# A decoder kernel whose instructions are recorded, list-scheduled on a model of the engines, and emitted in that order

## The chip, the cores and the metric

The kernel runs on one core of one Trainium2 chip. The metric is the device time of one execution in microseconds (us), the median of several runs. A profile of one execution goes with it. TensorE (PE) does the matmuls and loads their weights (PEld); VectorE (DVE), ScalarE (ACT) and GpSimd (POOL) do the elementwise work; SyncE (SP) and ScalarE issue the transfers (DMA). Every engine works through its own queue in order, and waits on semaphores for what other engines make.

## The reference

A trunk of two layers on x, 2048 tokens by 1024 channels. Layer 0 is a gated delta rule (GDN) with 8 heads, layer 1 gated linear attention (GLA) with 4 heads; in both a head has 128 key and 256 value channels. Cut to what matters:

```python
for i in range(DEPTH):                                   # 2 layers
    y = gdn_mixer(x, ...) if i % 2 == 0 else gla_mixer(x, ...)
    x = layer_norm(DEEP_ALPHA * x + y, ln_g[i], ln_b[i])

def gdn_mixer(x, w_in, conv_w, a_log, dt_bias, norm_w, w_out):
    p = x @ w_in                                         # q, k, v, gate, beta, decay
    qkv = causal_conv_silu(p[..., :GDN_QKV], conv_w)     # 4 taps
    ...                                                  # l2norm of q and k, beta, log decay g
    o = gated_delta_rule(q, k, v, g, beta)               # a triangular solve per chunk, a state per head
    o = gated_rmsnorm(o, norm_w, gate)                   # times silu(gate)
    return o.reshape(B, T, GDN_VAL) @ w_out
```

`gla_mixer` has the same frame: x @ w_in, a recurrence with a decay for every key channel, the gated norm, and w_out.

## The kernel before, in words

**Tiling.** Tokens are cut into four groups of 512 (`TG`), each of four chunks of 128. A *phase* is one layer on one group; `PHASES` puts them in the order (0,0) (0,1) (1,0) (0,2) (1,1) (0,3) (1,2) (1,3). A *unit* is one head of a phase: 32 units of GDN and 16 of GLA. Products with weights are made in full precision from two halves: a tile is split into a high part and the rest (`split`: a ScalarE cast, then a subtraction on VectorE, or on GpSimd for the input weights), and three matmuls (`mm3`) replace one.

**Stages of a unit.** The *GEMM* stage multiplies x (`xh`, `xl`, one set of 8 slots for a phase) by the head's columns of w_in, which stream as 128-row chunks (`wraw`, split into `wh`, `wl`), into PSUM banks `g` (three): q and k (`kq`), values (`vt`), gate (`sg`). GDN adds the short convolution, three multiply-adds on VectorE (`acc`). The *prep* stage makes the chunk-local matrices in PSUM banks `c` (three). In GDN it solves a triangular system: a 16x16 block step of some 30 small VectorE operations (`X`, `Xt`) on a tile `Arep`, which is `X` written to DRAM (`blk`) and read back replicated; then matmuls. The *chain* stage runs the recurrence over the four chunks, in bank `h` (one) and `c`, with the state `S` updated by VectorE. The *out* stage multiplies the normed result (`oT`, split into `oth`, `otl`) by the head's rows of w_out (`woraw`, split into `woh`, `wol`) in bank `o` (one, `pso` in the profile), and VectorE adds each product to `y`. After the last head of a phase comes the layer norm, and in layer 0 the transposed result is written for layer 1 (`x2T`).

**What sets the order.** The four stages are four generators (`chains`, `preps`, `outs`, `gemms`). `Plan` keeps rough costs (`COST`: each result 0.8 us late), and `Plan.run` takes, at each step, the first generator whose step is due by these. This sets the order of emission, which is the urgency that the framework's own scheduler goes by when it orders each engine's queue. By hand are: a gap between the output products (`O_GAP`), a delay for loading `y` (`Y_WAIT`), a loader of output weights that runs ahead (`prefetched`, `WO_AHEAD`), and loads of the next phase's x in the last gate GEMM (`free`). The raw tiles of output weights, of x and of the layer norm's vectors (`load_gb`) share four `woraw` buffers.

All instructions are issued through one helper, line 121, so the profile tells them apart by tiles.

Of the kernel before, what the change touches and what calls it, by code (L numbers as in the profile page):

```python
# [49 lines left out]
class Plan:  # L50
    """Decides the order of emission, which is the scheduler's order of urgency: a rough model of the engines says
    when a step's operands are there, and of the steps that could go, that of the first thread goes."""

    def __init__(self):
        self.clock = 0.0
        self.events = {}
        self.busy = dict.fromkeys("vsgd", 0.0)
        self.done, self.used, self.opens, self.slots = {}, {}, {}, {}

    def tile(self, tag, ap, bufs):  # L60
        slots = self.slots.setdefault(tag, [])
        slots.append(ap.tensor.name)
        self.opens[slots[-1]] = self.used.get(slots[-1 - bufs], 0.0) if len(slots) > bufs else 0.0

    def ready(self, *tiles):
        names = [t[:].tensor.name for t in tiles]
        return max(max(self.done.get(n, 0.0), self.opens.get(n, 0.0)) for n in names)

    def note(self, key, aps):
        dst, src = aps[0], aps[1:]  # L70
        names = [a.tensor.name for a in aps]
        t = max([self.opens.get(names[0], 0.0)] + [self.done.get(n, 0.0) for n in names[1:]])
        n = 1
        for k in (src[-1] if key == "t" else dst).shape[1:]:
            n *= k
        psum = any(a.space == PSUM for a in aps)
        if key == "t":
            m = 1
            for k in src[0].shape[1:]:
                m *= k  # L80
            rate = 0.6 if src[0].dtype == F32 else 2.4
            cost = m / 1.2 if src[0] is src[-1] else max(n / rate, m / rate, 107 if rate > 1 else 53)
            self.clock = end = max(self.clock, t) + cost
            end += COST["t"]
        else:
            if key == "d":
                cost, wait = COST["d"], COST["dw"] + 4 * n * P / 200
            else:
                fixed, each = COST[key]
                cost, wait = fixed + n * each, COST["w"]  # L90
            begin = max(self.busy[key], t)
            self.busy[key] = max(self.busy[key], min(begin, self.clock)) + cost
            end = begin + cost + wait
        self.done[names[0]] = max(end, self.done.get(names[0], 0.0))
        for a in names:
            self.used[a] = max(end, self.used.get(a, 0.0))

    def run(self, *threads, start):
        def due(th):
            return self.events.get(th[1], 1e30) if isinstance(th[1], tuple) else th[1]  # L100

        threads = [[t, t0] for t, t0 in zip(threads, start)]
        while threads:
            th = next((th for th in threads if due(th) <= self.clock), None) or min(threads, key=due)
            assert due(th) < 1e30
            self.clock = max(self.clock, due(th))
            try:
                th[1] = next(th[0])
            except StopIteration:
                threads.remove(th)  # L110


class Planned:
    def __init__(self, plan, engine, key):
        self.plan, self.engine, self.key = plan, engine, key

    def __getattr__(self, name):
        op = getattr(self.engine, name)

        def call(*args, **kw):  # L120
            ins = op(*args, **kw)  # L121
            aps = [a for a in (*args, *kw.values()) if isinstance(a, bass.AP)]
            if name == "transpose":
                aps = [aps[0], aps[1], aps[1]]
            self.plan.note(self.key, aps)
            return ins
        return call


COST = {"v": (110, 1.04), "s": (110, 0.84), "g": (90, 2.35), "w": 800, "t": 200, "d": 450, "dw": 2000}  # L130
# [3 lines left out]
def trunk(ctx, tc, x, xT, w_in1, conv, a_log, dt_bias, nw1, w_out1, w_in2, gk_up, gk_b, nw2, w_out2,  # L134
          ln_g, ln_b, consts, out, phases=None):
    nc = tc.nc
    plan = Plan()
    v, s, g = (Planned(plan, e, k) for e, k in ((nc.vector, "v"), (nc.scalar, "s"), (nc.gpsimd, "g")))
    pe, sync, acts = Planned(plan, nc.tensor, "t"), Planned(plan, nc.sync, "d"), Planned(plan, nc.scalar, "d")
    ready, events = plan.ready, plan.events  # L140
# [10 lines left out]
    def T(tag, shape, bufs=1, dt=F32, p=None):  # L151
        count[0] += 1
        t = (p or sb).tile(list(shape), dt, tag=tag, name=f"{tag}_{count[0]}", bufs=bufs)
        plan.tile(tag, t[:], bufs)
        return t
# [87 lines left out]
    def after(*names):  # L243
        for name in names:
            yield name

    def mark(*name):
        events[name] = plan.clock

    def prefetched(specs, load, ahead=1):  # L250
        ready = []
        specs = iter(specs)

        def take(ahead=ahead):
            while len(ready) <= ahead:
                spec = next(specs, None)
                ready.append(None if spec is None else load(spec))
            return ready.pop(0)
        return take

    class Stream:
        def __init__(self, specs):
            self.specs = iter(specs)
            self.chunks = {}
            self.taken = self.loaded = 0

        def load(self, freed):
            while self.loaded < freed + W_BUFS:
                spec = next(self.specs, None)
                if spec is None:  # L270
                    return
                w, cols, kc = spec
                raw = T("wraw", [P, 272], RAW_BUFS)
                n = 0
                for c0, cn, pair in cols:
                    rows = w[kc * P:(kc + 1) * P]
                    if pair:
                        sync.dma_start(raw[:, :2 * cn].rearrange("p (a b) -> p a b", a=2),
                                       rows[:, :2 * pair].rearrange("p (a b) -> p a b", a=2)[:, :, c0:c0 + cn])
                        n = 2 * cn  # L280
                    else:
                        sync.dma_start(raw[:, n:n + cn], rows[:, c0:c0 + cn])
                        n += cn
                h = T("wh", [P, 272], W_BUFS, F32R)
                l = T("wl", [P, 272], W_BUFS, F32R)
                split(h[:, :n], l[:, :n], raw[:, :n], g)
                self.chunks[self.loaded] = h, l
                self.loaded += 1

        def take(self):  # L290
            self.taken += 1
            return self.taken - 1, self.chunks.pop(self.taken - 1)
# [16 lines left out]
    def gemm(xs, group, lags, done, free=None):  # L309
        d, chunks = [None] * len(lags), {}  # L310
        for i in range(KC + lags[-1]):
            for a, lag in enumerate(lags):
# [5 lines left out]
                if a == 0:  # L318
                    chunks[kc] = W.take()
# [628 lines left out]
```

## Time and profile before

| | |
|---|---|
| median of 3 runs | 3253.45 us (3251.26 to 3255.64) |
| profiled execution, first to last instruction | 3246.0 us |
| median less the profiled span | 7.5 us |
| instructions | 55,989 |
| TensorE busy | 3064.1 us, 94% |
| VectorE busy | 2466.0 us, 76% |
| ScalarE busy | 1565.6 us, 48% |
| GpSimd busy | 1127.2 us, 35% |
| mean granted TensorE clock | 0.983 |
| read and written | 269.86 and 26.28 MB |

The profiled execution's own time is its span, and what lies around the span is taken from the median. A group of instructions is told as: line, engine, operation, out<-in by tile names, shapes, count | busy us, mean ns of one | idle time of its engine just before them, and what ended that. A wait is told as: engine and tile that waited <- engine and tile that ended the wait: us in total, times, longest. Matmuls overlap in the array, and their ends are modelled, so TensorE's busy time is not time at its peak; the spacing of their starts in the timeline shows the rate.

### The profile page before, as it was taken

Reading aid. Unit: us, or ns where it says so; the run is one execution under the profiler, and the core shown is the slowest. Engines: PE = TensorE matmul, PEld = TensorE weight load, DVE = VectorE, ACT = ScalarE, POOL = GpSimd, SP = SyncE. Lnnn points to the kernel's source line nnn. Section 1 sums busy time; section 2 is a strip of 40 time slices with the busy share of each in tenths; the row PEclk is TensorE's granted clock in tenths of the full one; section 3 lists DMA queues with packets and bytes.
Section 4 is the critical chain, followed back from the end, with each engine's and each line's share of the span. In section 5 each row is a group of like instructions: output and inputs, shape, how many; then the busy total and the mean of one; then the engine's idle time right before and its main releaser. Section 6 shows DMA issues by size and latency. Waiting matters only on the chain.

```text
span 3246.0 us, 55989 instructions
## 1 busy us (share of the span) xinstructions
PE 3064.1 (94%) x18430; PEld 2601.6 (80%) x18430; DVE 2466.0 (76%) x6345; ACT 1565.6 (48%) x4099; POOL 1127.2 (35%) x1506
## 2 busy tenths in 40 slices
PE   8899999989999999998999999999899999899997
PEld 7688778768888888877887888978778878798885
DVE  7677788787877687688778768677877786866677
ACT  5445444445444456444444545553444454465542
POOL 5333333333233234334233324432433322433341
PEclk9899999999999999999999999999999999999998
DMA  6222223242222315324222322532422232243231
GB/s 179 63 77 74 78 73 98 82 147 76 74 78 78 101 53 153 109 79 127 80 79 82 92 73 67 153 98 78 136 77 74 82 94 69 78 137 97 66 125 59
DMA packets 311604, 299.83 MB, mean 92 GB/s; under 512 B 40544, under 2 KB 253792, under 8 KB 311312
## 3 DMA queue, kind: packets, MB, share of 16 engines
q1 hardware_dynamic: 285200, 278.42, 30.0%
q10 hardware_dynamic: 26112, 17.83, 1.9%
q8 instruction: 145, 2.38, 0.3%
q14 instruction: 147, 1.20, 0.1%
HBM read 269.86 MB, written 26.28 MB: 91 GB/s over the span
## 4 chain that ended last, share of the span: by engine, by line
PE 47%; DVE 20%; DMA 7%; issue 2%; ACT 2%; POOL 0%; SPq 0%; DVEq 0%; ACTq 0%; POOLq 0%
PE psg L121 24%; PE psc L121 10%; PE pso L121 10%; DMA Arep<-blk 5%; PE psh L121 4%; DVE X L121 3%; DVE D L121 2%; DVE y L121 2%; DVE acc L121 2%; DVE Xt L121 2%; DVE lntmp L121 1%; DMA blk<-X 1%; DVE z L121 1%; DVE lnrs L121 1%; DVE lnst L121 1%
## 5 line engine op out<-in xcount | busy, mean ns | idle before, releaser
L121 POOL TENSOR_TENSOR wl<-wraw,wh 128x256 fp32r<-128x256 f32 x1152 | 950.0, 843 | 1349.7 <-ACT wh L121 1207.9
L121 ACT CAST wh<-wraw 128x256 fp32r<-128x256 f32 x1152 | 444.6, 405 | 373.9 <-PE psg L121 229.2
L121 PE MATMUL psg<-wh,xh 128*128 128x256 f32 (+1 forms) x2048 | 609.5, 298 | 12.8 <-ACT acc L121 6.1
L121 PE MATMUL psg<-wl,xh 128*128 128x256 f32 (+1 forms) x2048 | 586.4, 286 | 2.7 <-POOL wl L121 2.5
L121 PE MATMUL psg<-wh,xl 128*128 128x256 f32 (+1 forms) x2048 | 585.7, 286 | 0.0
L121 PE MATMUL psg<-xh,wh 128*128 128x512 f32 x1280 | 525.6, 411 | 2.9 <-DVE vt L121 1.3
L121 PE MATMUL psg<-xl,wh 128*128 128x512 f32 x1280 | 518.8, 405 | 0.6 <-DVE xl L121 0.6
L121 PE MATMUL psg<-xh,wl 128*128 128x512 f32 x1280 | 514.8, 402 | 0.1
L121 PEld LDWEIGHTS psg<-wh,xh 128*128 128x128 f32 x2048 | 392.6, 192 | 30.4 <-ACT acc L121 6.9
L121 PEld LDWEIGHTS psg<-wl,xh 128*128 128x128 f32 x2048 | 393.3, 192 | 16.5 <-POOL wl L121 3.8
L121 PEld LDWEIGHTS psg<-wh,xl 128*128 128x128 f32 x2048 | 392.9, 192 | 1.0
L121 PE MATMUL pso<-woh,oth 128*128 128x512 f32 x736 | 326.3, 443 | 61.7 <-DVE y L121 55.7
L121 DVE SCALAR_TENSOR_TENSOR acc<-pb,taps,acc 128x512 f32<-128x512 f32 x384 | 330.1, 862 | 44.4 <-ACT acc L121 39.1
L121 DVE SCALAR_TENSOR_TENSOR y<-pso,z,y 128x512 f32<-128x512 f32 x368 | 273.6, 743 | 111.7 <-PE pso L121 109.2
L121 PE MATMUL pso<-woh,otl 128*128 128x512 f32 x736 | 304.8, 414 | 12.9 <-DVE otl L121 11.5
L121 PE MATMUL pso<-wol,oth 128*128 128x512 f32 x736 | 298.6, 406 | 0.0
L121 PEld LDWEIGHTS psg<-xh,wh 128*128 128x128 f32 x1280 | 243.9, 191 | 56.1 <-DVE sg L121 3.2
L121 PEld LDWEIGHTS psg<-xh,wl 128*128 128x128 f32 x1280 | 242.7, 190 | 54.7 <-POOL wl L121 1.0
L121 PEld LDWEIGHTS psg<-xl,wh 128*128 128x128 f32 x1280 | 243.4, 190 | 53.4 <-DVE xl L121 2.5
L121 ACT ACTIVATE junk<-psc 128x128 bf16<-128x128 f32 (+1 forms) x448 | 144.2, 322 | 185.4 <-PE psc L121 150.8
L121 PEld LDWEIGHTS pso<-woh,oth 128*128 128x128 f32 x736 | 140.2, 190 | 100.9 <-DVE y L121 72.0
L121 DVE TENSOR_TENSOR Xt<-Arep,X 128x60 f32<-128x60 f32 (+14 forms) x480 | 131.9, 275 | 84.7 <-DMA Arep<-blk 76.6
(192 smaller groups left out, 5459.0 us busy)
## 6 DMA issues: line engine op xcount, KB each, us to landing
wraw<-in_w_in SPq DMA_DIRECT2D x1152, 128.0 KB, 2.3
woraw<-in_w_out SPq DMA_DIRECT2D x192, 256.0 KB, 3.6
Arep<-blk SPq DMA_DIRECT2D x32, 512.0 KB
woraw<-in_xT SPq DMA_DIRECT2D x32, 256.0 KB, 3.2
y<-in_x SPq DMA_DIRECT2D x16, 512.0 KB, 4.3
Gb<-gcT ACTq DMA_DIRECT2D x32, 256.0 KB, 3.0
x<-y SPq DMA_DIRECT2D x32, 256.0 KB, 2.1
x2T<-th ACTq DMA_DIRECT2D x32, 256.0 KB, 4.4
```

Of the source, the lines that this page charges most:

```text
L121: ins = op(*args, **kw)
```

## The change

`Plan` and the generators go. Every engine call is first only recorded (`Recorder.note`), as an operation with its tiles, its cost, its dependencies and a priority: the rank of its stage (chain, prep, out, GEMM, in this order), then the order of recording. A tile is a *slot* out of a fixed set for its tag, given at the first operation that uses it, or already at the load when that names it with `also`. `Recorder.place` runs a list scheduler: five engines (VectorE, ScalarE, GpSimd, TensorE, SyncE) with a clock each; the engine that can start earliest takes, of the operations that are ready and have their slots, the one of best priority. Operations that need a new slot wait when their unit lies more than `HORIZON` units ahead of the first unit whose chain is unfinished. `Recorder.emit` issues the operations in the order placed, and `linearize=True` has the framework keep this order. x gets its own raw tiles (`xraw`, two), the layer norm's vectors their own (`gb`, four). The stages become plain functions, called unit by unit; `O_GAP`, `Y_WAIT`, the stream and the loader that runs ahead go. The diff, cut:

```diff
+    def note(self, engine, key, name, args, kw, also):
+        op = Op()
...
+        op.prio, op.unit = (self.rank, op.at), self.unit
...
+        for v in also:
+            v.of.given = op
+            op.fresh.append(v.of)
+        self.cost(op, dst, every)
...
+    def cost(self, op, dst, every):
...
         if key == "t":
...
+            if op.name == "transpose":
+                op.cost = 2 * dst.shape[0] / 2.4 + 4
+            elif every[1].dtype == F32:
+                op.cost = 4 * mov / 2.4 + 9
+            else:
+                op.cost = mov / 2.25 + 4.5
+            op.lag = 210
+        elif key == "d":
+            size = 4 * n * dst.shape[0]
+            op.cost, op.lag = 430, 1700 + size / 170
...
+        elif key == "v":
+            n = max(n, max(size_of(a.shape) for a in every))
+            took = (150 if psum else 160) + 1.04 * n
+            if op.name == "scalar_tensor_tensor":
+                took += 55
+            if len(every) > 2 and not psum and n > 64:
+                took *= 1.12
+            op.cost, op.lag = took - 80, 80 + LAG
...
+            took = 140 + 2.8 * n if len(every) > 2 else 300 + n
+            op.cost, op.lag = took - 40, 40 + LAG
...
+    def place(self):
...
+            tag = "unit" if op.fresh and op.unit > front + HORIZON else blocked(op)
...
+            cost = op.cost
+            if op.func is not None and op.func != table[0]:
+                table[0], cost = op.func, cost + 1280
...
+            end = now + cost + op.lag
+            placed.append(op)
+            for u in op.users:
+                u.ready = max(u.ready, now + cost if u.deps[op] else end + (100 if u.key == "t" else 0))
...
+    def emit(self):
...
+        for op in self.place():
+            op.call(*[real(a) for a in op.args], **{k: real(a) for k, a in op.kw.items()})
...
-COST = {"v": (110, 1.04), "s": (110, 0.84), "g": (90, 2.35), "w": 800, "t": 200, "d": 450, "dw": 2000}
+LAG = 60
...
+        if tag not in rec.tags:
+            rec.tags[tag] = [p.tile([shape[0], n], dt, tag=f"{tag}_{k}", name=f"{tag}_{k}") for k in range(bufs)]
...
     def load_wo(spec, th="woh", tl="wol", bufs=None):
...
-            sync.dma_start(raw[:], w_out[r0:r0 + P, e * 512:(e + 1) * 512])
             hi = T(th, [P, 512], bufs, F32R)
             lo = T(tl, [P, 512], bufs, F32R)
+            sync.dma_start(raw[:], w_out[r0:r0 + P, e * 512:(e + 1) * 512], also=(hi, lo))
...
-    def gemm(xs, group, lags, done, free=None):
+    def gemm(u, specs, group, lags, done):
...
                 if a == 0:
-                    chunks[kc] = W.take()
-                at, (wh, wl) = chunks[kc]
-                yield ready(d[a], wl, xs[1][kc])
+                    if len(xs[0]) == kc:
+                        load_x(u, kc)
+                    chunks[kc] = chunk(specs[kc])
+                wh, wl = chunks[kc]
...
     def load_x(u, kc):
...
-        raw = T("woraw", [P, TG], WO_RAW_BUFS)
-        sync.dma_start(raw[:], x2T[u.gi][:, kc, :] if u.kind else xT[kc * P:(kc + 1) * P, u.t0:u.t0 + TG])
+        raw = T("xraw", [P, TG], 2)
         hi, lo = T("xh", [P, TG], KC, F32R), T("xl", [P, TG], KC, F32R)
+        sync.dma_start(raw[:], x2T[u.gi][:, kc, :] if u.kind else xT[kc * P:(kc + 1) * P, u.t0:u.t0 + TG],
+                       also=(hi, lo))
...
+    def gemms(u):
+        rec.rank = R_GEMM
+        if u.at == 0:
+            warm_up()
+            sync.dma_start(taps[:].rearrange("p a b -> p (a b)"), conv)
+            v.tensor_scalar(taps[:], taps[:], 0.5, None, ALU.mult)
+            setup()
...
+    def outs(u):
+        rec.rank = R_OUT
+        if u.first:
+            u.G["y"] = load_y((lambda n: x[u.t0 + n * P:u.t0 + (n + 1) * P, :]) if u.kind == 0
+                              else (lambda n: x2[u.gi][n][:]))
...
     def load_gb(u):
...
-                t = T("woraw", [P, 512], WO_RAW_BUFS)
+                t = T("gb", [P, 512], 4)
...
-    plan.run(chains(), preps(), outs(), gemms(), start=(0.0, 0.0, 1.0, 0.0))
+    for u in units:
+        rec.unit = u.at
+        gemms(u)
+        preps(u)
+        chains(u)
+        outs(u)
+    rec.emit()
...
-O_GAP = 7050
-Y_WAIT = 20000
+R_CHAIN, R_PREP, R_OUT, R_GEMM = range(4)
+HORIZON = 2
...
-    nc = bacc.Bacc("TRN2", target_bir_lowering=False, num_devices=1)
+    nc = bacc.Bacc("TRN2", target_bir_lowering=False, num_devices=1, dynamic_dma_scratch_size=1024)
...
-    with tile.TileContext(nc) as tc:
+    with tile.TileContext(nc, linearize=True) as tc:
```

676 lines of the change are left out of this document (364 added, 312 removed).

## The prediction

> **What bounds the kernel now.** The page first, for the share of each engine.
>
> ```profile
> span 3246.0 us, 55989 instructions
> PE 3064.1 (94%) x18430; PEld 2601.6 (80%) x18430; DVE 2466.0 (76%) x6345; ACT 1565.6 (48%) x4099; POOL 1127.2 (35%) x1506
> ```
>
> TensorE has work for 3064 of 3246 us. No order of the same 18,430 matmuls gets under that unless they themselves run faster, so the change can win the 182 us in which TensorE is idle, and the time in which it runs at a lower clock. The busy time by stretches (first 200 us, an ordinary stretch, a stretch with the end of a phase, the rest, the tail) says where the idle time lies.
>
> ```profile
> core 0: us, PE busy (x) PEld busy (x) DVE busy (x) ACT busy (x) POOL busy (x), PEclk, DMA share, GB/s
> 0.00:200.00 200.00, 174.58 (x941) 141.86 (x942) 144.18 (x348) 91.86 (x260) 76.76 (x112) 0.95 0.39 109
> 200.00:600.00 400.00, 388.07 (x2261) 321.40 (x2259) 311.57 (x803) 192.84 (x542) 133.41 (x199) 1.00 0.29 82
> 600.00:800.00 200.00, 180.76 (x1037) 149.79 (x1036) 159.49 (x452) 91.16 (x234) 76.30 (x102) 0.96 0.38 108
> 800.00:3200.00 2400.00, 2296.51 (x14090) 1969.62 (x14089) 1809.76 (x4632) 1179.91 (x3050) 831.36 (x1088) 0.99 0.32 92
> 3200.00:3246.00 46.00, 24.14 (x108) 18.94 (x106) 40.98 (x113) 9.80 (x15) 9.40 (x6) 0.81 0.19 69
> ```
>
> Idle: 200 - 174.6 = 25.4 at the start, 46 - 24.1 = 21.9 in the tail, and 11.9 + 19.2 + 103.5 = 134.7 between. VectorE is busy for 2466 us, 78% in the ordinary stretch, so it is no floor. Next TensorE's own waits and its granted clock, which belong together: the list of waits, the clock over the span, and a piece of TensorE's timeline (start, duration, tile; in brackets the idle time before).
>
> ```profile
> PE pso L121 <- DVE y L121: 60.8, 36, 5.4
> PE pso L121 <- DVE otl L121: 11.5, 10, 3.2
> PE psh L121 <- DVE S L121: 9.8, 5, 3.1
> ...
> PE psg L121 <- DVE sg L121: 8.6, 5, 4.4
> ...
> PE psh L121 <- DVE Rt L121: 1.7, 4, 0.5
> ```
>
> ```profile
> core 0: 3246.0 us, clock 0.983
> ```
>
> ```profile
> 1497.65 0.28 PE L121 MATMUL psg<-wh,xl 128*128 128x256 f32 x1
> 1500.36 0.39 PE L121 MATMUL psg<-wh,xh 128*128 128x256 f32 x1 [2.42 <-ACT acc L121]
> ...
> 1501.26 0.42 PE L121 MATMUL psg<-wh,xl 128*128 128x256 f32 x1
> 1501.47 0.41 PE L121 MATMUL psg<-wh,xh 128*128 128x256 f32 x1
> ...
> 1505.42 0.36 PE L121 MATMUL psg<-wh,xh 128*128 128x256 f32 x1
> 1505.62 0.28 PE L121 MATMUL psg<-wl,xh 128*128 128x256 f32 x1
> 1505.74 0.28 PE L121 MATMUL psg<-wh,xl 128*128 128x256 f32 x1
> ```
>
> Three things are to be seen. The waits are few and long: 36 of 1.7 us for the one bank `pso`, which `y`'s update on VectorE has to empty. A wait is paid twice: after an idle 2.42 us the same matmul starts every 0.21 us (1501.26 to 1501.47) where 0.12 is normal (1505.62 to 1505.74). And a change of group costs: the first matmul after a foreign group takes 0.20 (1505.42 to 1505.62) instead of 0.12. The mean clock of 0.983 puts the loss to the low clock at 0.017 x 3246 = 55 us, of which (1 - 0.95) x 200 = 10 lie in the first 200 us and (1 - 0.81) x 46 = 9 in the tail; 36 are left for the middle.
>
> The Trainium skill ("TensorE: Matmul & The Clock Gate", Part 1) has the clock fall after an idle window of about 3.4 us, so that its rule is to avoid TensorE gaps longer than that. The trace shows the slow stretch after 2.42 us. By the rule nearly none of the listed waits would cost clock, and the forecast below would be some 29 us higher; the timeline decides, and I keep the term.
>
> **The change part by part.** The instructions stay the same in kind and number: same matmuls, splits, loads. What changes is the order on each engine's queue, and when buffers are handed on. The order was made by an emission plan with rough costs (every result 0.8 us late) and then by the framework's own scheduler; now a list scheduler places each instruction on the engine where it could start first, by rank (chain, prep, out, GEMM), and that order is final.
>
> (1) *Waits in the middle.* The new costs against rows of this trace:
>
> ```profile
> L121 DVE SCALAR_TENSOR_TENSOR acc<-pb,taps,acc 128x512 f32<-128x512 f32 x384 | 330.1, 862 | 44.4 <-ACT acc L121 39.1 <-POOL halo L121 1.5
> L121 DVE SCALAR_TENSOR_TENSOR y<-pso,z,y 128x512 f32<-128x512 f32 x368 | 273.6, 743 | 111.7 <-PE pso L121 109.2 <-issue 1.5
> L121 POOL TENSOR_TENSOR wl<-wraw,wh 128x256 fp32r<-128x256 f32 x1088 | 887.6, 833 | 1267.7 <-ACT wh L121 1128.5 <-PE psc L121 48.6 <-PE psg L121 35.6
> ```
>
> The new formulas give (160 + 1.04 x 512 + 55) x 1.12 = 838 ns for `acc` (862 measured), 150 + 532 + 55 = 737 for `y` (743), 140 + 2.8 x 256 = 857 for `wl` (833); a 256-wide `psg` matmul gets 256/2.25 + 4.5 = 118 ns, the 0.12 of the timeline. With costs within 3% the model knows when the one `o` bank is free, and GEMM work, which has the lowest rank and is nearly always there, goes in the place of the wait. What it cannot cover is where GEMM work itself lacks operands: phase changes (the 600 to 800 us stretch loses 19.2 in 200, the ordinary one 11.9 in 400). Ends of the range: none of the 134.7 us won, or all. I take 80%, between the `pso` wait, which should vanish, and the chain's hand-offs, which stay: -108 us. The rest, 27 us, is the new order's own lateness.
>
> (2) *Clock.* It goes with the waits: 80% of 36 = -29 us (0 to -36).
>
> (3) *The start.* The rank decides on SyncE's queue too. All loads without an earlier user are ready at once, and those of the out stage (rank 2) go ahead of the GEMM's (rank 3): four `y`, four `woraw`, then the constants of `setup`, and only then x and w. Before, it was x and w first:
>
> ```profile
> 0.74 0.44 SPq L121 DMA_DIRECT2D wraw<-in_w_in  x1
> 1.24 0.45 SPq L121 DMA_DIRECT2D woraw<-in_xT  x1
> ```
> ```profile
> 5.53 1.06 PE L121 MATMUL psg<-xh,wh 128*128 128x512 f32 x2
> ```
> ```profile
> woraw<-in_w_out SPq DMA_DIRECT2D x192, 256.0 KB, 3.6
> Arep<-blk SPq DMA_DIRECT2D x32, 512.0 KB
> woraw<-in_xT SPq DMA_DIRECT2D x32, 256.0 KB, 3.2
> y<-in_x SPq DMA_DIRECT2D x16, 512.0 KB, 4.3
> ...
> cst<-in_consts SPq DMA_DIRECT2D x1, 704.0 KB
> ```
>
> Ahead of x stand 4 x 512 + 4 x 256 + 704 KB = 3.9 MB. 256 KB more take 4.3 - 3.2 = 1.1 us (`y` against `woraw<-in_xT`), so some 240 GB/s and 16 us, in which TensorE has nothing else: +16 us (0, if packets of all loads share the engines so that x comes soon, to +22, at the 179 GB/s that the page's first slice moved). The model gives each load its own latency and no shared bandwidth, so it does not see this.
>
> (4) *Buffers.* x gets its own two raw buffers and the layer norm's `gb` its own four; both took `woraw` before. Same 64 and 32 loads, no cost; what it frees is the wait for output weights at the end of a phase, seen in the chain that ended last:
>
> ```profile
> 1520.40 5.39 DMA woraw<-in_w_out
> ...
> 1541.27 1.44 DMA blk<-X
> 1542.73 6.93 DMA Arep<-blk
> ```
>
> That piece (5.39 us) reaches TensorE through `woh`, and belongs to the 134.7 already counted: 0 more. Against it stands `also=(hi, lo)`: a load of x or of output weights is now issued only when the slots of its split are free, where it needed a raw buffer alone. For the output weights the cover is the rest of the unit. For x it is the end of the last gate GEMM: a slot of x comes free with the last of four token tiles, and a landing of 3.2 us and the split (about 1.5) fit into the 11 groups of three matmuls that remain after the first (11 x 3 x 0.117 = 3.9 us) but for about 1 us. Seven changes of phase: +7 us (0 to 7 x 3.2 = +22, with that cover gone).
>
> (5) *`Arep`.* The model prices its landing at 0.43 + 1.7 + 3.1 = 5.2 us; the chain shows 6.93. VectorE will stand at the first `Xt` for 1.7 us in 32 units, and everything behind it on VectorE's queue waits, GEMM evacuations too. Before, the same wait was there (76.6 us over 32, in the waits of `Xt`), so 0 against now, up to +54 if TensorE's three `g` banks fill meanwhile.
>
> (6) *Without cost:* the horizon of two units, which the two buffers of `kq`, `vt` and `sg` set anyway; O_GAP, Y_WAIT and the prefetch counter go (waits of the plan, no instructions); the last unit's `oT` uses `oth`/`otl` instead of `D1`/`D2` (those are free by then); the ACT table loads depend on the order:
>
> ```profile
> L121 ACT ACT_TABLE_LOAD x33 | 42.3, 1283 | 18.9 <-DVE Gb L121 14.9 <-DVE ztmp L121 2.8 <-PEq L938 0.7
> ```
>
> Twice as many would be 42 us more on ScalarE, which is 48% busy: hidden, 0 to +10. The smaller DMA scratch only makes room. The tail (21.9 us idle) is VectorE's layer norm and stays.
>
> Sum: 3246 - 108 - 29 + 16 + 7 = 3132 us of span. The profiled execution's span stands 7.5 us under the median of the runs, 3253.45; with that, **3140 us**.
>
> **The rivals.** *Slower: hand-offs run late.* Now LAG is 60 ns (plus 100 towards TensorE) where the plan had 800. An order built to the edge puts a chain matmul at the very instant its operand should come; queues run in order, so TensorE then stands in front of it with GEMM work behind. The kernel has about 1,660 such hand-offs (16 in the chain, some 14 in prep, 10 in out for each of 32 units, about 24 for each of 16). The forecast's gain of 114 us is gone at a mean lateness of 114/1660 = 0.07 us beyond what is allowed for. For it speaks the weight-load queue of now:
>
> ```profile
> PEld psh L121 <- ACT wt L121: 23.8, 97, 0.5
> PEld psh L121 <- DVE S L121: 21.6, 37, 3.5
> ```
>
> 45.4 us over the chain's 512 hand-offs is 0.09 us each; against it, on the matmuls themselves only 9.8 + 1.7 us are left, 0.02 each. At 0.12 us: 3132 + 199 + 7 = 3338 us.
>
> *Given back.* Waits move from `pso` to the phase changes and to `Arep`: half of the waits and clock come (-54 - 15), start +16, phases +15, `Arep` +10: 3246 - 28 + 7 = 3225 us. The costs within 3% speak against it, the loads without bandwidth for it.
>
> *Nearly all is won.* 134.7 + 36 go, start +10, and fewer changes of group (0.08 us each): 3246 - 171 + 10 - 20 + 7 = 3072 us or less.
>
> *The flag does more than order.* If the total order is kept with waits from one engine to the next, no two engines overlap, and the time is at least the sum of the busy times: 3064 + 2466 + 1566 + 1127 = 8223 us. Nothing in the diff asks for that, but nothing in this trace can exclude it.
>
> **How the numbers follow.** Forecast 0.55 (its own range 3080 to 3195); nearly all won 0.09; given back 0.13; no difference, within 0.2% (6.5 us, about what this measurement can tell from none), 0.05; late hand-offs 0.13; order by waits 0.05. Faster: 0.55 + 0.09 + 0.13 = 0.77; same 0.05; slower 0.18. The range 3050 to 3290 takes in the first four but for some 0.03 below, and a third of the late hand-offs: it leaves out 0.03 + 0.09 + 0.05 = 0.17.
>
> **What would show it.** Right: `pso` waits for `y` well under 60.8 us, TensorE idle between 200 us and the tail near 30, mean clock about 0.99, first `psg` matmul with x after 15 us or later with `y` loads at the head of SyncE's queue. Wrong: many short waits before `psh` and `psc` (late hand-offs); TensorE's busy time far from 3064 (then changes of group, not waits, made the difference); idle time gathered at phase changes; or instructions of different engines that hardly overlap.

## The result and the profile after

The changed kernel takes 19063.74 us (median, 19062.94 to 19071.47); the kernel before took 3254.55 us beside it. The ratio is 5.855, 95% interval 5.847 to 5.863. The forecast was 3140 us. The rival to which it gave a chance of 0.05, that the order is kept by waits from one engine to the next, is what happened, and its lower bound of 8223 us was less than half of the time.

First the page of the changed kernel and its mean clock, in the order span, busy time by engine, clock.

```profile
span 19061.5 us, 58843 instructions
PE 8476.1 (44%) x18430; PEld 4308.3 (23%) x18430; DVE 2549.2 (13%) x6345; ACT 1743.4 (9%) x4099; POOL 967.7 (5%) x1506
...
core 0: 19061.5 us, clock 0.520
```

The numbers of matmuls and of VectorE, ScalarE and GpSimd operations are those of before. The busy times of TensorE, VectorE, ScalarE and GpSimd add up to 8476.1 + 2549.2 + 1743.4 + 967.7 = 13,736 us, less than the span. Before, they added up to 8223 us in a span of 3246. So before, two or three engines worked at any moment; now, on average, fewer than one does. A piece of the timeline shows it instruction by instruction (start, duration, engine, instruction; in brackets the engine's idle time before it and what ended that).

```profile
8999.48 0.58 ACT L345 COPY pb<-psg 128x512 f32<-128x512 f32 x1 [4.30 <-PE psg L345]
...
9000.12 0.80 PE L345 MATMUL psg<-xl,wh 128*128 128x512 f32 x1 [0.73 <-ACT pb L345]
9000.95 0.71 DVE L345 STREAM_TRANSPOSE U<-Tm 128x512 f32<-128x512 f32 x1 [3.71 <-PE psg L345]
...
9001.72 0.80 PE L345 MATMUL psg<-xh,wl 128*128 128x512 f32 x1 [0.80 <-DVE U L345]
9002.58 0.37 SPq L345 DMA_DIRECT2D wraw<-in_w_in  x1
...
9004.74 0.79 PE L345 MATMUL pso<-woh,oth 128*128 128x512 f32 x1 [2.22 <-DMA wraw<-in_w_in]
9005.57 0.69 ACT L345 ACTIVATE acc<-psg,taps 128x512 f32<-128x512 f32 x1 [5.50 <-PE pso L345]
9006.32 0.19 POOL L345 COPY pb<-halo 128x3 f32<-128x3 f32 x1 [8.20 <-ACT acc L345]
```

Read the starts against the ends. 8999.48 + 0.58 is 9000.06, and the matmul starts at 9000.12; it ends at 9000.92, and VectorE starts at 9000.95; that ends at 9001.66, and the next matmul starts at 9001.72. One instruction runs at a time. The names show that no data is handed over: a matmul of the gate GEMM (`psg<-xh,wl`) waits for a transpose of the triangular solve (`U`), and a matmul of the out stage (`pso<-woh,oth`) waits 2.22 us for a transfer of input weights (`wraw`) that it does not read. Even the landing of a transfer is waited for by whatever comes next in the list. The list of waits says the same in sums (engine and tile that waited, what it waited for, us in total, times, longest):

```profile
POOL wl L345 <- PE psg L345: 4799.2, 350, 118.0
...
PE psg L345 <- DMA wraw<-in_w_in: 1294.3, 472, 14.4
...
PE psc L345 <- DMA wraw<-in_w_in: 412.5, 157, 5.8
...
PE pso L345 <- DMA wraw<-in_w_in: 331.6, 126, 4.0
```

GpSimd's `wl` reads `wraw` and `wh` only, and yet waits 4799 us for `psg` of TensorE (35.6 before, in the row of `wl` that the prediction shows). TensorE alone stands 1294.3 + 412.5 + 331.6 = 2038 us behind landings of `wraw`, which no matmul reads. Besides the waits, TensorE's own work got slower. The same group of matmuls, in the kernel before and in the changed one (count, busy us, mean ns):

```profile
L121 PE MATMUL psg<-xh,wh 128*128 128x512 f32 x1280 | 525.6, 411 | 2.9 <-DVE vt L121 1.3
```
```profile
L345 PE MATMUL psg<-xh,wh 128*128 128x512 f32 x1280 | 964.1, 754 | 1423.5 <-DMA wraw<-in_w_in 305.0
```

754 ns against 411, at a mean clock of 0.520 against 0.983. The trace tells the clock and the pauses apart: after a pause of over 0.3 us, a matmul of this group takes 498 ns where the record has the full clock (13 of them) and 794 where it has half (821). 881 of the 1280 start after such a pause, so, as an estimate, some 60 of the 343 ns more come from the pauses and the rest from the clock. Of the 15,815 us that were added to the span, 8476 - 3064 = 5412 lie in longer TensorE time; the other 10,403 are TensorE's idle time, 10,585 us where it was 182.

### The profile page after: what moved, and what is told of

Read it like the earlier page. It is cut to its first block, busy times and chain, and to the rows that moved or that the text cites. A ratio compares the mean times of both kernels' runs of the same rounds, so it can differ in the third digit from the quotient of the medians.

```text
span 19061.5 us, 58843 instructions
## 1 busy us (share of the span) xinstructions
PE 8476.1 (44%) x18430; PEld 4308.3 (23%) x18430; DVE 2549.2 (13%) x6345; ACT 1743.4 (9%) x4099; POOL 967.7 (5%) x1506
## 5 line engine op out<-in xcount | busy, mean ns | idle before, releaser
L345 PE MATMUL psg<-xh,wh 128*128 128x512 f32 x1280 | 964.1, 754 | 1423.5 <-DMA wraw<-in_w_in 305.0
L345 PE MATMUL psg<-xh,wl 128*128 128x512 f32 x1280 | 966.2, 756 | 1270.3 <-DMA wraw<-in_w_in 333.5
L345 PE MATMUL psg<-xl,wh 128*128 128x512 f32 x1280 | 967.6, 756 | 1142.2 <-DMA wraw<-in_w_in 163.4
L345 PE MATMUL psg<-wh,xl 128*128 128x256 f32 (+1 forms) x2048 | 1015.2, 499 | 1021.4 <-ACT wh L345 150.9
L345 PE MATMUL psg<-wh,xh 128*128 128x256 f32 (+1 forms) x2048 | 1002.2, 490 | 956.9 <-DMA wraw<-in_w_in 165.0
L345 PE MATMUL psg<-wl,xh 128*128 128x256 f32 (+1 forms) x2048 | 988.6, 483 | 763.2 <-DMA wraw<-in_w_in 153.1
L345 PEld LDWEIGHTS psg<-wh,xl 128*128 128x128 f32 x2048 | 625.0, 307 | 1344.3 <-ACT wh L345 196.4
L345 PEld LDWEIGHTS psg<-wh,xh 128*128 128x128 f32 x2048 | 633.1, 309 | 1268.5 <-DMA wraw<-in_w_in 180.5
L345 PEld LDWEIGHTS psg<-wl,xh 128*128 128x128 f32 x2048 | 636.9, 311 | 1035.4 <-DMA wraw<-in_w_in 175.4
L345 PE MATMUL pso<-wol,oth 128*128 128x512 f32 x736 | 540.2, 734 | 683.6 <-DMA woraw<-in_w_out 179.0
```

What stands on the lines that cost most here:

```text
L345: op.call(*[real(a) for a in op.args], **{k: real(a) for k, a in op.kw.items()})
```

## The experiments

### The flag and the order apart

Three kernels tell the flag and the order apart. The first keeps the order of the changed kernel on each engine's own queue and nothing else: the flag goes, and each instruction gets an edge without a semaphore to the one before it on the same engine. In the traces, the operations of TensorE, VectorE, ScalarE and GpSimd come in the same order in both kernels.

```diff
-    with tile.TileContext(nc, linearize=True) as tc:
+    with tile.TileContext(nc) as tc:
...
+        order = mybir.DependencyInfo(mybir.DependencyClass.NoSync, mybir.DependencyReason.DATA)
...
+                if ins.engine in last:
+                    tc.add_manual_dep(ins, last[ins.engine].name, order, reason="order")
+                last[ins.engine] = ins
```

> Same order on every engine's queue as the changed kernel, instruction for instruction, but kept by edges between neighbours on one engine alone (no semaphore), with the total-order flag off. Theory A (the flag makes every instruction wait for the one before it, whatever its engine): the engines overlap again, the sum of busy times is far above the span, and the time falls from 19064 us to what the blind prediction gave for the order itself, 3140 us (3050 to 3290), with the first GEMM matmul after 15 us or later. Theory B (the placed order itself is at fault: hand-offs late, loads at the wrong place): the time stays above 10000 us.

The second only drops the flag, so that the framework's scheduler goes by the recorded order as urgency; the third is the kernel before with the flag (`TileContext(nc, linearize=True)`) and nothing else.

> The changed kernel with the flag alone taken out: the recorded order is now only the urgency that the framework's own scheduler goes by. Theory A: engines overlap, 3100 to 3350 us, a little above the kernel with the exact order, since the framework's scheduler moves instructions by costs of its own. Theory B: the bad order is partly kept, so clearly above the kernel before, over 3400 us.

> The kernel before with the flag alone put in; nothing of the recorder or the list scheduler. Theory A: no two engines overlap, so at least the sum of busy times of before, 8223 us, and with half the matmul rate and every load's landing in the open some 15000 to 22000 us, like the changed kernel. Theory B (the flag only keeps the order of emission): 3200 to 3700 us.

| kernel | us | ratio to before |
|---|---|---|
| placed order per engine, no flag | 3511.97 | 1.078 [1.076, 1.080] |
| no flag, framework's scheduler | 3512.06 | 1.079 [1.077, 1.081] |
| kernel before with the flag | 16171.26 (one run) | 4.97 (one run) |

The flag is the cause of the 19,064 us, from both sides: taking it out while the order on each engine is kept brings 15,552 us back, and putting it into the kernel before costs 12,916 us there. The page of the latter shows the same picture, with more span than the 5975.5 + 2548.4 + 1743.3 + 967.6 = 11,235 us of work:

```profile
span 16169.5 us, 56366 instructions
...
PE 5975.5 (37%) x18430; PEld 4008.5 (25%) x18430; DVE 2548.4 (16%) x6345; ACT 1743.3 (11%) x4099; POOL 967.6 (6%) x1506
```

But the order itself is 7.8% slower than the one before, where the forecast had it 3.5% faster. That it comes out the same under the framework's scheduler shows that the strictness of the order is not what costs. The page of the order-only kernel, its clock, and TensorE's waits:

```profile
span 3514.7 us, 55902 instructions
...
PE 3157.8 (90%) x18430; PEld 2646.6 (75%) x18430; DVE 2551.7 (73%) x6345; ACT 1568.0 (45%) x4099; POOL 1096.0 (31%) x1506
```
```profile
core 0: 3514.7 us, clock 0.961
...
PE pso L347 <- DVE y L347: 61.5, 46, 4.2
PE psc L347 <- DVE U L347: 43.8, 21, 3.3
PE psc L347 <- DVE og L347: 32.3, 29, 2.9
PE psg L347 <- DVE acc L347: 22.2, 10, 7.8
PE psg L347 <- DVE sg L347: 21.2, 12, 2.5
```

TensorE's idle time is 3514.7 - 3157.8 = 357 us against 182, and the low clock takes (1 - 0.961) x 3514.7 = 137 us against 55: 175 + 82 = 257 of the 269 us that the span grew. The wait of `pso` for `y`, which the forecast had vanish, stands at 61.5 (60.8 before), and new ones stand in front of prep and chain matmuls (`psc`) and of the GEMM (`psg`). Summed over the whole lists of the two kernels, TensorE's waits grew from 25.6 to 114.3 us in front of `psg`, from 37.1 to 104.9 in front of `psc`, from 15.7 to 30.3 in front of `psh`, and hardly in front of `pso` (78.2 and 80.6). It is not a matter of single places. The stretches that the prediction shows as ordinary and as a phase change (duration; busy us of TensorE, its weight loads, VectorE, ScalarE, GpSimd; clock, DMA share, GB/s):

```profile
200.00:600.00 400.00, 361.24 (x2013) 295.51 (x2012) 290.76 (x745) 164.71 (x457) 115.01 (x174) 0.96 0.29 73
600.00:800.00 200.00, 172.60 (x969) 141.84 (x969) 153.43 (x395) 91.25 (x243) 72.72 (x98) 0.93 0.37 105
```

388.07 became 361.24 in the ordinary stretch, 180.76 became 172.60 in the other.

### Room for lateness, prices, rank

All kernels from here on have the order-only form, with a change in the plan alone. The first four: `LAG = 200` instead of 60 (slack); the GEMM stage's loads, splits, evacuations and convolution ahead of all else (feeders first); two prices of the plan (priced); the last two together. `LAG` is part of the price of every result of VectorE, ScalarE and GpSimd, not of a matmul or a transfer.

```diff
-LAG = 60
+LAG = 200
```
```diff
-        op.prio, op.unit = (self.rank, op.at), self.unit
+        op.prio, op.unit = (-1 if self.rank == R_GEMM and key != "t" else self.rank, op.at), self.unit
```
```diff
+            op.multi = op.name == "transpose" or every[1].dtype == F32
...
-            op.cost, op.lag = took - 80, 80 + LAG
+            op.cost, op.lag = 1.15 * took - 80, 80 + LAG
...
+            if op.key == "t":
+                if multi[0] and not op.multi:
+                    cost += 190 if op.cost > 200 else 105
+                multi[0] = op.multi
```

> The placed order, kept per engine only, with one number of the plan changed: LAG 200 ns instead of 60, so that every result counts as 140 ns later. The order-only kernel took 3512 us. Theory 'too tight' (work comes a little later than placed, and every engine then stands in front of it): 140 ns of room for each result covers many of the short waits for VectorE (U 43.8, og 32.3, S 16.6 us), so 3350 to 3450 us. Theory 'wrong prices' (some classes cost much more than placed, the rest is right): an equal allowance for all helps less, 3430 to 3500. Theory 'rank' (the work that feeds the GEMM comes last on VectorE, ScalarE and GpSimd, and so TensorE lacks GEMM work to fill waits with): no help, 3490 to 3530. If the plan's tightness cost nothing, the allowance would make it slower than 3530.

> The placed order, kept per engine only, with one change of rank: the GEMM stage's loads, splits, evacuations and convolution go ahead of everything else; its matmuls stay last. Theory 'rank': TensorE waits for acc, sg, wh, vt, wl in front of GEMM matmuls (84 us in the order-only kernel's list) and has none to fill the waits of chain and prep with; both go down, so 3350 to 3450 us. Theories 'too tight' and 'wrong prices': these waits go, but the chain's and prep's own operations come later on VectorE, so that it about cancels: 3480 to 3540.

> The placed order, kept per engine only, with two prices of the plan changed: every VectorE operation 1.15 times as long, and 190 ns more for the first 512-wide matmul (105 for a narrower one) of three-part products behind a full-precision matmul or a transpose. The order-only kernel's trace has both: the first 512-wide matmul behind such a one is followed after 416 ns where 231 is normal. Theory 'wrong prices': the placed times then agree with the chip's, the short waits of psc and psh for VectorE fall to less than half, 3360 to 3440 us. Theory 'too tight': much the same as more LAG does. Theory 'rank': 3490 to 3530.

> Both changes together: the prices of VectorE and of a change of matmul kind, and the GEMM stage's loads, splits and evacuations ahead of all else. If prices and rank are separate causes, the gains add up: from 3512 by what each alone gives, to 3220 to 3300 us, near the kernel before (3254). If they are one cause seen twice, it comes out no better than the better one of the two, 3350 to 3440. If neither is the cause, above 3450.

| kernel | us | ratio to before |
|---|---|---|
| slack, LAG 200 | 3330.44 | 1.022 [1.020, 1.024] |
| feeders first | 3397.63 | 1.042 [1.039, 1.044] |
| priced | 3510.29 | 1.077 [1.074, 1.080] |
| priced and feeders first | 3312.77 | 1.016 [1.014, 1.018] |

Slack alone wins 182 of the 256 us between the order-only kernel and the kernel before, more than was expected of it. The rank alone wins 114, as the theory of the rank had it. The two prices alone do nothing, against the theory that wrong prices are the cause; together with the rank they add 85 us to what the rank gives, which no theory had. The page of the slack kernel:

```profile
span 3328.0 us, 55961 instructions
...
PE 3091.5 (93%) x18430; PEld 2607.9 (78%) x18430; DVE 2474.5 (74%) x6345; ACT 1560.1 (47%) x4099; POOL 1085.0 (33%) x1506
...
core 0: 3328.0 us, clock 0.977
```

Idle 236 us and 0.023 x 3328.0 = 77 us of low clock: 120 and 60 less than in the order-only kernel, which together are 181 of the 187 us between the two spans.

### Which room it is, and how much

`LAG` acts in three ways: on users on other engines, on the release of buffers, and on users on the same engine. The next two kernels give the 140 ns to the first two or to the third only. A third has `LAG = 400`, and a fourth joins LAG 200 and feeders first.

```diff
+            left = end + (140 if op.key in "vsg" else 0)      # between only: the release of buffers
...
+                room = 140 if op.key in "vsg" and u.key != op.key else 0      # between; within: u.key == op.key
+                u.ready = max(u.ready, now + cost if u.deps[op] else end + room + (100 if u.key == "t" else 0))
```

> Of the 140 ns that the kernel with LAG 200 added to every result, only what concerns another engine: users on another engine, and the release of a buffer. Users on the same engine keep LAG 60. With all of it the time went from 3512 to 3330 us. Theory 'tight hand-offs' (TensorE stands in front of a matmul whose operand on VectorE or ScalarE is a little late): nearly all of the gain is here, 3320 to 3370 us. Theory 'own chains' (on VectorE a dependent instruction was placed right behind the one it needs, and other work would have fitted between): hardly any, 3460 to 3520.

> The other half: 140 ns more only where the user is on the same engine as the maker; other engines' users and buffers keep LAG 60. Theory 'own chains': nearly all of the gain is here, 3320 to 3380 us, and the small VectorE operations of the triangular solve (X and Xt, 278 and 290 ns in the order-only kernel, 250 and 241 with LAG 200) are short again. Theory 'tight hand-offs': 3460 to 3520.

> LAG 200 and the GEMM stage's loads, splits and evacuations ahead of all else. Alone they gave 182 and 114 us. If they cure different waits, the gains add up but for what overlaps: 3230 to 3290 us, about the kernel before (3254 to 3260). If both only give TensorE more GEMM work ready, whichever way, it comes out like the better one: 3310 to 3340.

> LAG 400 alone. The plan of the kernel before counted each result 0.8 us late; if room for lateness is what the new plan lacks, 340 ns more do at least as well as 140 (3330): 3260 to 3340 us. If 140 ns was the right size of the chip's lateness, more of it delays the chain in the plan and so leaves TensorE with GEMM work exhausted at the ends of phases: 3340 to 3450.

So many waits changed that a control was due: does the greedy placement scatter by this much when next to nothing is changed? Three kernels have LAG 70, 190 and 220, and a fourth joins feeders first, the prices and the room within an engine.

> LAG 70 instead of 60, 10 ns, which is far under any lateness that the traces show: a control. If the named causes act, the time stays within 15 us of the 3512 at LAG 60. If the greedy placement scatters (one instruction placed otherwise shifts all that follow), it lands anywhere from 3400 to 3560, and differences of that size between the other variants prove nothing.

> LAG 190, a control beside the 3330 us at LAG 200. Named causes: 3315 to 3350. Scatter: anywhere from 3300 to 3480.

> LAG 220, the control on the other side of 200. Named causes: 3315 to 3355, with a slow rise towards the 3509 at LAG 400. Scatter: anywhere from 3300 to 3480.

> Three changes together: GEMM feeders first, the two prices, and 140 ns more for users on the same engine (alone 3398, 3510 and 3398 us; the first two together 3313). If they are separate causes: 3210 to 3290 us, at or under the kernel before. If they cure the same waits or the placement scatters: 3300 to 3400.

| kernel | us | ratio to before |
|---|---|---|
| LAG 60 (order-only kernel) | 3511.97 | 1.078 [1.076, 1.080] |
| LAG 70 | 3503.40 | 1.076 [1.075, 1.078] |
| LAG 190 | 3341.26 | 1.027 [1.026, 1.028] |
| LAG 200 | 3330.44 | 1.022 [1.020, 1.024] |
| LAG 220 | 3362.23 | 1.033 [1.031, 1.035] |
| LAG 400 | 3508.73 | 1.079 [1.077, 1.081] |
| 140 ns more, between engines and for buffers only | 3480.43 | 1.071 [1.069, 1.074] |
| 140 ns more, within an engine only | 3398.47 | 1.045 [1.043, 1.047] |
| LAG 200, feeders first | 3358.22 | 1.033 [1.031, 1.035] |
| feeders first, priced, 140 ns within | 3612.88 | 1.110 [1.109, 1.112] |

The controls land within 9, 11 and 32 us of their neighbours (LAG 220 is 7 us above what was expected of it), so the time scatters by up to some 30 us here: differences under that say nothing, and those of 100 us and more are well outside it. Along `LAG` the time has a valley: too little room costs 180 us, and too much of it as much again.

Three plans lie well outside everything that was expected of them. LAG 400 is one. LAG 200 with feeders first is 28 us slower than LAG 200 alone, though each helped by itself. And the last row joins three changes that alone gave 114, 2 and 114 us, two of which together gave 199: all three cost 101. The gains do not add up, so what one change gives is its worth in this plan and not the size of a cause.

Of the 182 us, room within an engine gives 114 by itself and room between engines 32, about what a control moves (the rest needs both). So 140 ns more for the hand-offs from engine to engine is not what was missing. The waits of `psc` show what the two kinds of room changed. Kernel with room between engines, then kernel with room within:

```profile
PE psc L349 <- DVE og L349: 29.3, 15, 2.7
PE psc L349 <- DVE U L349: 27.8, 14, 3.1
```
```profile
PE psc L348 <- DVE og L348: 12.1, 37, 1.6
...
PE psc L348 <- DVE U L348: 3.9, 8, 1.2
```

43.8 + 32.3 = 76.1 us of TensorE's waits for `U` and `og` become 57.1 with room between the engines and 16.0 with room within. `U` ends the run of some 30 dependent small VectorE operations of the triangular solve. One end of such a run in the order-only kernel, VectorE first, then TensorE at the same time:

```profile
301.09 0.16 DVE L347 TENSOR_TENSOR Xt<-Arep,X 128x8 f32<-128x8 f32 x1
301.28 0.17 DVE L347 TENSOR_TENSOR X<-X,Xt 128x8 f32<-128x8 f32 x1
301.49 0.17 DVE L347 TENSOR_TENSOR Xt<-Arep,X 128x4 f32<-128x4 f32 x1
301.69 0.58 DVE L347 TENSOR_TENSOR X<-X,Xt 128x4 f32<-128x4 f32 x1
302.30 0.69 DVE L347 TENSOR_TENSOR Tm<-X,cst 128x512 f32<-128x512 f32 x1
303.02 0.71 DVE L347 STREAM_TRANSPOSE U<-Tm 128x512 f32<-128x512 f32 x1
```
```profile
300.19 0.50 PE L347 MATMUL psg<-xh,wh 128*128 128x512 f32 x1 [2.50 <-DVE sg L347]
...
300.99 0.40 PE L347 MATMUL psg<-xh,wh 128*128 128x512 f32 x1
303.79 1.22 PE L347 MATMUL psc<-U,D 128*128 128x128 f32 x4 [2.40 <-DVE U L347]
```

The small operations follow one another every 0.2 us with hardly anything between, and TensorE stands twice: for `sg`, an evacuation of the GEMM that VectorE did late, and for `U`. In the traces one can count what VectorE does between the first `Xt` and the `Tm<-X,cst` of each of the 32 runs, and how long after the end of the transpose that makes `U` the first matmul that reads it starts (means):

| kernel | length of the run, us | other VectorE operations inside it | from `U` to its matmul, us |
|---|---|---|---|
| before | 14.6 | 18.5 | 9.41 |
| order-only (LAG 60) | 15.3 | 9.4 | 0.20 |
| room between engines | 14.5 | 9.2 | 0.31 |
| room within an engine | 19.7 | 15.6 | 0.55 |
| LAG 200 | 19.6 | 17.8 | 0.59 |
| priced | 18.5 | 13.6 | 0.28 |
| feeders first | 15.3 | 12.0 | 0.19 |

With 60 ns of room the chain of the solve, which has the better rank, takes VectorE nearly for itself; with 140 ns more the plan finds other work for the holes, and the matmul that needs `U` is placed later. The kernel before does as much other work in a shorter run, and the last column has a larger difference: it leaves 9.4 us between `U` and its use, so a late `U` stops nothing, where the placed orders use it at once.

That the packed runs are the cause is argued, not shown. The priced kernel has longer runs with more other work in them, and takes 3510 us; feeders first has short ones, and takes 3398; and the kernel without the flag waits only 11.5 us for `U`, in the same 3512 us. A rival is untested as well. The plan prices the landing of `Arep` at 5.2 us, where a row that the prediction shows has 6.93, and VectorE stood 54.7 us at the first `Xt`, 2.0 us in each of 27 runs, about as long as TensorE then stood for `U` (43.8 us, 2.1 in each of 21). Room within an engine, 140 ns for each of some 30 steps, adds up to 4 us for a run and would cover that, and 140 ns between engines would not. No run changes this one price.

```profile
DVE Xt L347 <- DMA Arep<-blk: 54.7, 27, 3.8
```

Too much room is another matter. In the kernel with LAG 400 the short `psc` waits are not what stands out:

```profile
PE psg L347 <- DVE acc L347: 116.1, 30, 7.2
PE psg L347 <- DVE vt L347: 33.1, 20, 2.8
```

TensorE stands in front of GEMM matmuls for 116.1 us (22.2 in the order-only kernel), until VectorE has done the convolution `acc` that empties the way: work of the lowest rank, which comes ever later.

### Three last ones

Is that the price of too much room? LAG 400 with feeders first; LAG 200 with the price for a change of matmul kind only; and LAG 200 with the out stage's first loads moved behind the GEMM's:

```diff
+        late = not self.unit and self.rank == R_OUT and key == "d"
+        op.prio, op.unit = (R_LATE if late else self.rank, op.at), self.unit
```

> LAG 400 with the GEMM stage's loads, splits and evacuations ahead of all else. LAG 400 alone took 3509 us, and TensorE waited 116.1 us for acc, 33.1 for vt in front of GEMM matmuls. If that, the GEMM's evacuations standing behind everything else on VectorE, is what too much LAG costs, these waits fall under 40 us and the time to 3330 to 3400 us. If too much LAG costs by leaving the chain late at the ends of units: 3450 to 3530.

> LAG 200 and the price for a change of matmul kind (190 ns before 512-wide ones, 105 before narrower ones); VectorE's prices as they were. LAG 200 alone: 3330 us. If the unpriced first matmuls make the order late, pricing them gives a further 20 to 70 us: 3260 to 3310. If LAG 200 covers them already, or a price does not change what is placed: 3315 to 3360.

> LAG 200, and the loads of y and output weights of unit 0 behind the GEMM stage's loads. With them in front, the first matmul with x starts at 18.72 us, where the kernel before has 5.53. If the start is on the path that sets the end, the 13 us come off: 3310 to 3325 us. If later work takes the delay up (the out stage, which now has its loads later): 3325 to 3340.

| kernel | us | ratio to before |
|---|---|---|
| LAG 400, feeders first | 3567.25 | 1.095 [1.093, 1.098] |
| LAG 200, kinds priced | 3412.95 | 1.048 [1.046, 1.049] |
| LAG 200, start loads behind | 3329.16 | 1.022 [1.021, 1.023] |

The first came out as neither theory said. In the kernel with LAG 400 and feeders first the wait for `acc` is gone as expected, and other waits take its place:

```profile
PE psg L347 <- ACT wh L347: 69.1, 19, 6.5
PE psh L347 <- ACT wt L347: 39.5, 84, 0.7
PE psg L347 <- DVE acc L347: 33.3, 12, 5.8
```

`acc` was thus where TensorE stood, but not the cause of the 180 us; what is remains open. The price for a change of kind makes the order with LAG 200 83 us slower, where 20 to 70 us of gain or no change was expected. With the rank the prices helped, here one of them harms, and why is open. And the start is taken up by later work. The first matmul with x, in the order-only kernel and with the loads behind:

```profile
18.76 1.22 PE L347 MATMUL psg<-xh,wh 128*128 128x512 f32 x2 [13.29 <-ACT wh L347]
```
```profile
10.16 1.22 PE L348 MATMUL psg<-xh,wh 128*128 128x512 f32 x2 [4.88 <-ACT xh L348]
```

8.6 us earlier at the start, and no difference that can be told at the end (3329.16 against 3330.44).

None of the versions beats the kernel before. The best, priced and feeders first, is 1.6% slower. What holds the last 1.6 to 2.2% is open: its idle time is 3312.2 - 3097.7 = 215 us against 182.

## Why the prediction was wrong, point by point

**The reading of the flag** is the step that failed. The prediction, and the description of the change before it, took "the framework keeps this order" to mean the order on each engine's queue, and put the whole sum on that. It keeps one order over all engines, by waits. The sign that the prediction named for this, "instructions of different engines that hardly overlap", is the timeline above. The rival had the mechanism, and mis-sized it by a factor of 2.3: its bound was the sum of the busy times of before, but one at a time those grow (TensorE from 3064 to 8476 us, at half the clock and without pipelining), and 19,061.5 - 13,736 = 5325 us more lie between the instructions, in hand-offs and in landings that nothing covers. A chance of 0.05 for the worst outcome by far, on a keyword that no row of the profile can tell about, was the poorest judgement in it.

**(1) Waits in the middle**, -108 us: wrong also for the order alone, where TensorE's idle time grew by 175. The step from "costs within 3%" to "the model covers the waits" failed. Prices that are right for single classes of instructions did not make the order right: `pso` waited 61.5 us instead of vanishing, and the new waits lay in front of the GEMM (89 us more) and of prep and chain (68 and 15 more). How they come about is open; the plan that packs the dependent operations on VectorE and uses `U` at once is the nearest reading.

**(2) Clock**, -29 us: right that it goes with the waits, and so wrong in sign: from 55 to 137 us lost in the order-only kernel.

**(3) The start**, +16 us: the queue was read rightly (`x` stood behind `y` and `woraw`, first matmul with x at 18.76 us, where 15 or more was said, 13.2 us later than before), but the sum took this as lost. Moving the loads gained nothing at the end.

**(4), (5) and (6)**, +7, 0 and 0: the losses do not gather at phase changes (27 us in 400 of the ordinary stretch, 8 in 200 of the other), so what belongs to phase changes, (4), is small. The table loads of (6) stayed at 33 in the order-only kernel. For (5), VectorE's stand at the first `Xt` was read rightly, 54.7 us in all, less than the 76.6 before; whether TensorE pays for it, which the sum put at 0, is the open rival above. None of the three was tried by itself.

**Late hand-offs**, 3338 us: nearest for the order alone, with the right sign, but the order-only kernel's 3512 lies (3512 - 3140) / (3338 - 3140) = 1.9 times as far above the forecast, which would be 0.22 us for each hand-off instead of 0.12; and 140 ns between engines did not cure it: that room gave 32 us, room within an engine 114.

## What to carry to other kernels

A switch that "keeps the order" has two meanings, order on each queue and order over all engines, and the price between them was a factor of 5.4 here; when a change turns on one, its meaning is the first thing to settle, and afterwards ten lines of the timeline do. A static order needs room for lateness: 140 ns more for each result was worth 5%, and 340 ns more was worth nothing, so this is a number to tune on the chip and not to derive. Look for that room in the runs of dependent instructions on one engine as well as in hand-offs, measure from traces how long a result lies ready before its use (9.4 us for `U` before, 0.2 in the placed order), and time a control with a trivial change before reading causes from small differences between two schedules.

## What the runs showed of the hardware

TensorE ran at half its clock for nearly all of the 19 ms although it was busy for 44% of the time. In the piece between 9000 and 9012 us no pause that is shown is longer than 2.22 us, and the clock of that window is half:

```profile
9000.00:9012.00 12.00, 4.77 (x7) 1.93 (x7) 1.46 (x2) 1.16 (x3) 0.37 (x2) 0.50 0.06 17
```

The records of the clock begin 636 us into the span, and what lies before counts as full in the mean. It was not: a matmul of `psg<-xh,wh` after a pause takes 794 ns there, as long as under a recorded half clock. From there on the trace has the full clock 27 times, for 3.4 to 10.2 us each, 116 us in all. Here are the 3.4 us before one of these times, the 3.4 us of full clock, the 3.4 us behind, and a matmul in the second, 0.50 us where the one at 9001.72 took 0.80:

```profile
9302.19:9305.60 3.41, 3.17 (x12) 2.47 (x10) 0.20 (x1) 0.00 (x0) 0.00 (x0) 0.50 0.00 0
9305.60:9309.02 3.42, 1.55 (x9) 0.83 (x10) 1.24 (x2) 0.41 (x1) 0.00 (x0) 0.99 0.00 0
9309.02:9312.43 3.41, 1.60 (x17) 1.09 (x15) 0.71 (x1) 0.00 (x0) 0.72 (x1) 0.51 0.00 0
```
```profile
9306.15 0.50 PE L345 MATMUL psg<-xh,wh 128*128 128x512 f32 x1 [0.78 <-DVE U L345]
```

All 27 are alike: in the 3.4 us before, TensorE was busy for 84% or more, and in the time at full clock for 32 to 60%, after which it was half again. Work in single instructions thus rarely fills a stretch well enough to get the full clock, and does not keep it.

The Trainium skill ("TensorE: Matmul & The Clock Gate", Part 1) has a low clock after an idle window of about 3.4 us and the full one again only after such a window of sustained work. The second half agrees with this trace, by the 27 times above. The first half does not: the clock fell again each time, and the longest pause of TensorE within the 27 times at full clock was 2.3 us.
